# Hybrid encoder block on one core: second token half's transposes placed among the output products of the last chunks, row norms one chunk behind, the last chunk's mixer output gated later

## The chip, the cores and the metric

One core of a Trainium2 chip runs the kernel. The metric is the device time of one execution in microseconds, the median of several runs. The kernel before took 1236.85 us (median of 3 runs, 1236.0 to 1237.21). The trace and the profile page come from one further, profiled execution of the same kernel, which took 1241.54 us.

## The reference, cut to what matters

One layer of an encoder with 1024 tokens of width 1024. Two groups of heads (windowed attention, and gated DeltaNet run forwards and backwards over the tokens) read one normalised input; their outputs are joined, multiplied by `W_out` and added to the input, which gives `h`. Then a feed-forward with a squared ReLU, and a last norm.

```python
attn = _windowed_gqa(...)                       # 8 heads of 64
gdn  = _gdn_mixer(...)                          # rmsnorm(o_fwd + o_bwd) * silu(z), 4 heads of 128
h = h + jnp.concatenate([attn, gdn], axis=-1) @ w_out[l]
hn = _rmsnorm(h, norm_ffn_w[l])
h = h + jnp.square(jax.nn.relu(hn @ w_ffn_in[l])) @ w_ffn_out[l]
return _rmsnorm(h, norm_final_w)
```

## The kernel before

Tokens are handled in 8 chunks of 128, and in two halves of 512: chunks 0 to 3 are the first half, chunks 4 to 7 the second. The kernel is built by a Python class whose generators are woven together. A scheduler in the tile framework then fixes the order of the instructions on each engine once, when the kernel is built; on the chip each engine runs its own list in order and waits at semaphores. Weights and activations are split into a high and a low part, so each product of 128 by 512 takes three matmuls (`mm3`, L125 to L129).

The place of the change is the joint between the mixers and the feed-forward:

- The backward scan (L811 to L862) runs over the chunks from 7 down to 0. When a chunk's scan is done, it is in `self.scanned`.
- `out_gdn(c)` (L905) makes the DeltaNet operand of a chunk: it squares the scan's output by head on ScalarE (L914), turns the sums into a factor on VectorE (L916 to L919) and GpSimd (a power, L920), multiplies (VectorE, L921), transposes four blocks on TensorE (L924, into a `psA` bank), gates with `z` (VectorE, L925) and splits the result in two parts (ScalarE L122, GpSimd L123).
- `out_gemm` (L883) multiplies a chunk's operand by `W_out`: two halves of 12 matmuls each, in a `psA` bank each, and VectorE adds each half to `h[c]` (L890).
- `out_all` (L930) runs over the chunks 7 to 0, keeps up to three chunks' operands ready ahead, and stores `h[c]` to HBM (L940). Chunks are named by their row buffer in listings below.
- `norm_h(c)` (L946) normalises a chunk's row for the feed-forward through `norm_rows` (L199): the square and its sum on ScalarE (L204, 1024 elements), two small operations on GpSimd (L191, L192), and a multiplication on VectorE (L206). The rows of chunks 4 to 7 are scaled in place, after their store to HBM.
- `tokens_second` (L973) normalises chunks 7 to 4 (`norm_half(1)`), and then transposes the second half: for each of 8 blocks of columns, four transposes on TensorE (L210) into one `psB` bank (`token_block`, L954), which ScalarE and VectorE read out as operands (L986, L215, L216, L990, L968, L969). It is woven with the rest of `out_all` once four chunks are summed (L1324).
- After that come the early products of the feed-forward (`early`, L1099: 24 matmuls from the operands of the second half) and `tokens_first` (L999), which transposes the normalised rows of chunks 0 to 3 (L210 again, with `sc` rows) and makes the operands of the first half.
- `psA` and `psB` are two rotations of four PSUM banks each.

Of the kernel before, what the change touches and what calls it, by code (L numbers as in the profile page):

```python
# [22 lines left out]
GH = 4  # L23
# [54 lines left out]
class Block:  # L78
# [46 lines left out]
    def mm3(self, ps, wh, wl, xh, xl, first, last, onto=False):  # L125
        nc = self.nc
        nc.tensor.matmul(ps, wh, xh, start=first, stop=False, skip_group_check=onto)  # L127
        nc.tensor.matmul(ps, wh, xl, start=False, stop=False, skip_group_check=onto)  # L128
        nc.tensor.matmul(ps, wl, xh, start=False, stop=last, skip_group_check=onto)  # L129

# [752 lines left out]
    def out_gemm(self, h, mh, ml, wo):  # L883
        nc = self.nc
        for nh in range(2):
            sl = slice(nh * HALF, (nh + 1) * HALF)
            ps = self.ps("psA")
            for j, k in enumerate((3, 0, 1, 2)):
                self.mm3(ps, mh[:, k, :], ml[:, k, :], wo[k][0][:, sl], wo[k][1][:, sl], j == 0, j == 3)
            nc.vector.tensor_tensor(out=h[:, sl], in0=h[:, sl], in1=ps, op=ALU.add)  # L890
# [14 lines left out]
    def out_gdn(self, c):  # L905
# [16 lines left out]
        ps = self.ps("psA", (P, GH, P))  # L922
        for h in range(GH):
            nc.tensor.transpose(ps[:, h, :], zc[:, 1, h, :], self.ident)  # L924
        nc.vector.scalar_tensor_tensor(out=mix, in0=ps, scalar=self.w_gdn, in1=zc[:, 0], op0=ALU.mult, op1=ALU.mult)  # L925
# [4 lines left out]
    def out_all(self, chunks):  # L930
        while len(self.wo[1]) < 4:
            yield 0.5
        ready = []
        for n, c in enumerate(chunks):
            while c not in self.scanned:
                yield 0.5
            while len(ready) < 3 and n + len(ready) < len(chunks) and chunks[n + len(ready)] in self.scanned:
                ready.append(self.out_gdn(chunks[n + len(ready)]))
            yield from self.out_gemm(self.h[c], *ready.pop(0), self.wo[1])
            self.nc.sync.dma_start(out=self.hd[c], in_=self.h[c])  # L940
            self.summed.append(c)
            if c < 4 and len(self.rows) >= 4:
                self.norm_h(c)

# [9 lines left out]
    def token_block(self, rows, k):  # L954
        ps = self.ps("psB")
        for i in range(4):
            self.transpose_row(rows[i], i, ps, k)
        return ps
# [14 lines left out]
    def tokens_second(self):  # L973


        nc = self.nc
        self.norm_half(1)
        yield 5.0
        rows = [self.rows[4 + i] for i in range(4)]
# [296 lines left out]
    def phases(self):  # L1276
# [40 lines left out]
        def output():  # L1317
# [4 lines left out]
            while len(self.summed) < 4:  # L1322
                yield next(out)
            yield from weave((out, 20.0), (self.tokens_second(), 9.0))  # L1324

# [73 lines left out]
```

## Time and profile before

| what | us |
|---|---|
| median of 3 runs | 1236.85 (1236.0 to 1237.21) |
| the profiled execution | 1241.54 |
| span of its trace | 1239.7 |
| TensorE busy in the span | 1178.8 (95%) |
| VectorE, ScalarE, GpSimd busy | 856.8, 611.3, 560.7 |

The span is the time from the first to the last instruction on the core; the profiled execution is 1.8 us longer than it. TensorE is the busiest engine by far, so what lengthens the program is time in which TensorE waits or runs at a lowered clock. A row of the timeline gives the start in us, the duration in us, the engine, the line, the operation, the tiles written and read, their sizes, how many instructions it merges and, in brackets, how long the engine sat idle before it and what it waited for. A row of the windows gives the stretch, its length, the busy time of each engine with its number of instructions, then the clock that TensorE was granted (1.00 is full), the DMA share and the GB/s.

### The profile page before, as it was taken

Reading aid. Unit: us, or ns where it says so; the run is one execution under the profiler, and the core shown is the slowest. Engines: PE = TensorE matmul, PEld = TensorE weight load, DVE = VectorE, ACT = ScalarE, POOL = GpSimd, SP = SyncE. Lnnn points to the kernel's source line nnn. Section 1 sums busy time; section 2 is a strip of 40 time slices with the busy share of each in tenths; the row PEclk is TensorE's granted clock in tenths of the full one; section 3 lists DMA queues with packets and bytes.
Section 4 is the critical chain, followed back from the end, with each engine's and each line's share of the span. In section 5 each row is a group of like instructions: output and inputs, shape, how many; then the busy total and the mean of one; then the engine's idle time right before and its main releaser. Section 6 shows DMA issues by size and latency. Waiting matters only on the chain. (4 is left out here: it accounts for less than half of the span.)

```text
span 1239.7 us, 18446 instructions
## 1 busy us (share of the span) xinstructions
PE 1178.8 (95%) x6482; PEld 964.3 (78%) x6482; DVE 856.8 (69%) x1482; ACT 611.3 (49%) x1331; POOL 560.7 (45%) x470
## 2 busy tenths in 40 slices
PE   7999999899889999897899999999999999999997
PEld 5788878677768878786788888888777888888885
DVE  4676667993489986776755354453677797887976
ACT  5455688334376761215554454554555433444343
POOL 5354312223321243233673544535446555665595
PEclk9999999899999999999999999999999999999999
DMA  6134344533646576222144434444688624443323
GB/s 241 52 101 144 99 171 143 176 101 112 205 146 184 163 265 248 68 94 91 54 140 158 144 145 159 147 153 144 221 274 298 225 87 155 150 140 133 99 88 136
DMA packets 121629, 187.62 MB, mean 151 GB/s; under 512 B 11043, under 2 KB 64416, under 8 KB 121537
## 3 DMA queue, kind: packets, MB, share of 16 engines
q1 hardware_dynamic: 103876, 155.20, 38.3%
q10 hardware_dynamic: 17661, 31.24, 6.7%
q8 instruction: 51, 0.84, 0.3%
q14 instruction: 41, 0.34, 0.1%
HBM read 122.39 MB, written 63.49 MB: 150 GB/s over the span
## 5 line engine op out<-in xcount | busy, mean ns | idle before, releaser
L127 PE MATMUL psA<-pg,wh 128*128 128x512 f32 x416 | 165.8, 399 | 3.5 <-DVE pt L482 1.9
L129 PE MATMUL psA<-pg,wl 128*128 128x512 f32 x416 | 165.1, 397 | 0.0
L128 PE MATMUL psA<-pg,wh 128*128 128x512 f32 x416 | 165.0, 397 | 0.0
L1174 DVE TENSOR_TENSOR pg<-pg 128x512 fp32r<-128x512 f32 x112 | 121.0, 1114 | 24.8 <-ACT pg L1173 24.8
L123 POOL TENSOR_TENSOR wl<-wr,wh 128x512 fp32r<-128x512 f32 x44 | 66.3, 1527 | 157.3 <-ACT wh L122 129.5
L123 POOL TENSOR_TENSOR wh<-wr,wh 128x512 fp32r<-128x512 f32 x32 | 47.4, 1503 | 128.9 <-ACT wh L122 128.9
L128 PE MATMUL psA<-pg,pg 128*128 128x512 f32 x256 | 100.5, 394 | 2.3 <-POOL pg L123 2.2
L129 PE MATMUL psA<-pg,pg 128*128 128x512 f32 x256 | 100.5, 393 | 0.0
L127 PE MATMUL psA<-pg,pg 128*128 128x512 f32 x256 | 99.6, 394 | 0.9 <-DVE pg L1219 0.8
L1091 ACT ACTIVATE pt<-pt 128x512 f32<-128x512 f32 x64 | 40.3, 632 | 120.6 <-DVE pt L1081 120.6
L123 POOL TENSOR_TENSOR pg<-wr,pg 128x512 fp32r<-128x512 f32 x48 | 72.5, 1540 | 52.7 <-ACT pg L122 48.8
L127 PEld LDWEIGHTS psA<-pg,wh 128*128 128x128 f32 x416 | 79.3, 191 | 21.3 <-ACT pt L464 2.1
L128 PEld LDWEIGHTS psA<-pg,wh 128*128 128x128 f32 x416 | 79.1, 190 | 18.1 <-issue 0.9
L129 PEld LDWEIGHTS psA<-pg,wl 128*128 128x128 f32 x416 | 79.1, 190 | 16.9
L1173 ACT CAST pg<-pg 128x512 fp32r<-128x512 f32 x112 | 67.3, 620 | 40.8 <-DMA pg<-sd 29.3
L128 PE MATMUL psB<-pg,pg 128*128 128x512 f32 x192 | 75.0, 391 | 0.8 <-POOL pg L123 0.7
L129 PE MATMUL psB<-pg,pg 128*128 128x512 f32 x192 | 74.8, 390 | 0.0
L127 PE MATMUL psB<-pg,pg 128*128 128x512 f32 x192 | 74.8, 390 | 0.0
L122 ACT CAST wh<-wr 128x512 fp32r<-128x512 f32 x76 | 43.6, 622 | 52.0 <-PE psA L128 32.0
L1081 DVE TENSOR_TENSOR pt<-psB,pt 128x512 f32<-128x512 f32 x39 | 26.9, 689 | 54.0 <-PE psB L129 29.5
L1081 DVE TENSOR_TENSOR pt<-psA,pt 128x512 f32<-128x512 f32 x39 | 26.8, 689 | 51.7 <-PE psA L129 36.3
L128 PEld LDWEIGHTS psA<-pg,pg 128*128 128x128 f32 x256 | 48.4, 189 | 13.5 <-POOL pg L123 3.7
(395 smaller groups left out, 3244.3 us busy)
## 6 DMA issues: line engine op xcount, KB each, us to landing
sd<-pt ACTq DMA_DIRECT2D x112, 256.0 KB, 2.0
pg<-sd SPq DMA_DIRECT2D x112, 256.0 KB, 2.9
wr<-in_w_ffn_in SPq DMA_DIRECT2D x32, 512.0 KB, 3.6
wr<-in_w_in SPq DMA_DIRECT2D x22, 512.0 KB, 4.8
pg<-in_x SPq DMA_DIRECT2D x16, 512.0 KB, 6.2
wr<-in_w_ffn_out SPq DMA_DIRECT2D x16, 512.0 KB, 4.4
sc<-kvd SPq DMA_DIRECT2D x14, 512.0 KB, 4.1
kvd<-pt SPq DMA_DIRECT2D x16, 256.0 KB, 2.4
```

Source lines behind the costliest of these rows:

```text
L122: nc.scalar.copy(out=h, in_=raw)
L123: (eng or nc.gpsimd).tensor_tensor(out=l, in0=raw, in1=h.bitcast(F32), op=ALU.subtract)
L127: nc.tensor.matmul(ps, wh, xh, start=first, stop=False, skip_group_check=onto)
L128: nc.tensor.matmul(ps, wh, xl, start=False, stop=False, skip_group_check=onto)
L129: nc.tensor.matmul(ps, wl, xh, start=False, stop=last, skip_group_check=onto)
L1081: self.nc.vector.tensor_tensor(out=out, in0=in0, in1=in1, op=ALU.add)
L1091: self.nc.scalar.activation(out=c, in_=c, func=AF.Relu)
L1173: nc.scalar.copy(out=s[:, 0], in_=raw)
L1174: v.tensor_tensor(out=s[:, 1], in0=raw, in1=s[:, 0].bitcast(F32), op=ALU.subtract)
```

## The change

Five edits, all at this joint:

1. `mm3` hands back its last matmul, and `out_gemm` keeps the last matmul of each product it has written in `self.summing`.
2. The transposes of `out_gdn` and those of `token_block` stand in a block that puts them, in TensorE's order alone, behind that last matmul (`issue_after`; on one engine the order is enough, and no semaphore is added).
3. `out_all` normalises the chunk summed before just ahead of a chunk's product, for all chunks. Before, `tokens_second` normalised chunks 7 to 4 in one go, and chunks 3 to 1 were normalised right behind their own sum.
4. `out_all` prepares chunk 0 only while fewer than two operands are ready (three for the other chunks).
5. A new generator `out_and_tokens` takes the place of the weave: behind each half product it takes 0, 1, 2, 2, 2 and 1 steps of `tokens_second`, then the rest. A step is one or the other `token_block` of a pair.

```diff
@@ out_gemm
             for j, k in enumerate((3, 0, 1, 2)):
-                self.mm3(ps, mh[:, k, :], ml[:, k, :], wo[k][0][:, sl], wo[k][1][:, sl], j == 0, j == 3)
+                m = self.mm3(ps, mh[:, k, :], ml[:, k, :], wo[k][0][:, sl], wo[k][1][:, sl], j == 0, j == 3)
+            self.summing = m.ins
@@ out_gdn
-        for h in range(GH):
-            nc.tensor.transpose(ps[:, h, :], zc[:, 1, h, :], self.ident)
+        with self.tc.issue_after(self.summing):
+            for h in range(GH):
+                nc.tensor.transpose(ps[:, h, :], zc[:, 1, h, :], self.ident)
@@ out_all
-        ready = []
-        for n, c in enumerate(chunks):
+        ready, coming = [], list(chunks)
+        for c in chunks:
             while c not in self.scanned:
                 yield 0.5
-            while len(ready) < 3 and n + len(ready) < len(chunks) and chunks[n + len(ready)] in self.scanned:
-                ready.append(self.out_gdn(chunks[n + len(ready)]))
+            while coming and coming[0] in self.scanned and len(ready) < (3 if coming[0] else 2):
+                ready.append(self.out_gdn(coming.pop(0)))
+            if self.summed:
+                self.norm_h(self.summed[-1])
             yield from self.out_gemm(self.h[c], *ready.pop(0), self.wo[1])
             self.nc.sync.dma_start(out=self.hd[c], in_=self.h[c])
             self.summed.append(c)
-            if c < 4 and len(self.rows) >= 4:
-                self.norm_h(c)
+    def out_and_tokens(self, out):
+        tokens, blocks = self.tokens_second(), iter((0, 1, 2, 2, 2, 1))
+        for v in out:
+            yield v
+            if v > 1:
+                yield from itertools.islice(tokens, next(blocks, 0))
+        yield from tokens
@@ token_block
-        for i in range(4):
-            self.transpose_row(rows[i], i, ps, k)
+        with self.tc.issue_after(self.summing):
+            for i in range(4):
+                self.transpose_row(rows[i], i, ps, k)
@@ tokens_second
-        self.norm_half(1)
-        yield 5.0
         rows = [self.rows[4 + i] for i in range(4)]
@@ output
-            yield from weave((out, 20.0), (self.tokens_second(), 9.0))
+            yield from self.out_and_tokens(out)
```

Below are TensorE's rows at the last of the eight column blocks of the second half, before. The `pg` names are the rows of chunks 4, 5, 6 and 7; the L924 row is the four transposes of chunk 0, and the L127 row opens chunk 2's product.

```order
L210 MATMUL psB_6121<-ident,pg_5192 128x128
L210 MATMUL psB_6121<-ident,pg_5096 128x128
L210 MATMUL psB_6121<-ident,pg_5007 128x128
L210 MATMUL psB_6121<-ident,pg_4904 128x128
L924 MATMUL psA_5941<-ident,wr_5926 128x128 x4
L127 MATMUL psA_5951<-pg_5155,pt_5801 128x512
```

Before, all eight blocks stand in one run of 32 transposes, with chunk 0's transposes behind them, and the products of chunks 2, 1 and 0 only after that. In the changed kernel the first block stands between the two halves of chunk 2's product:

```order
L129 MATMUL psA_5925<-pg_4970,pt_5816 128x512
L210 MATMUL psB_5940<-ident,pg_5192 128x128
L210 MATMUL psB_5940<-ident,pg_5096 128x128
L210 MATMUL psB_5940<-ident,pg_5007 128x128
L210 MATMUL psB_5940<-ident,pg_4904 128x128
L127 MATMUL psA_5946<-pg_5155,pt_5815 128x512
```

The other seven blocks follow behind the later half products: two behind chunk 2's second half, two behind each half of chunk 1, one behind chunk 0's first half. Chunk 0's own transposes stand behind the first of these pairs, ahead of chunk 1's product.

The next place is TensorE's list at the transposes of chunk 1, before. The first row ends chunk 4's product, L924 is chunk 1's transposes, the L811 rows are the last of the scan, and the last row opens chunk 3's product.

```order
L129 MATMUL psA_5819<-pg_4970,pt_5691 128x512
L924 MATMUL psA_5850<-ident,wr_5835 128x128 x4
L811 MATMUL psB_5478<-sc_5429,pt_5431 128x128 x2
L811 MATMUL psB_5482<-sc_5340,pg_3716 128x128 x2
L811 MATMUL psB_5487<-sc_5429,pt_5431 128x128 x2
L127 MATMUL psA_5860<-pg_5155,pt_5746 128x512
```

In the changed kernel the scan's rows have moved ahead of chunk 4's product, and chunk 1's transposes (L926 now) stand directly between the two products:

```order
L128 MATMUL psA_5840<-pg_4971,pt_5691 128x512
L129 MATMUL psA_5840<-pg_4970,pt_5692 128x512
L926 MATMUL psA_5871<-ident,wr_5856 128x128 x4
L127 MATMUL psA_5888<-pg_5155,pt_5753 128x512
L128 MATMUL psA_5888<-pg_5156,pt_5753 128x512
```

The third place is VectorE's list for the same transposes, before. `sm` is the small tile of chunk 1's factor, `pg_5096` and `pg_5192` are the rows of chunks 5 and 4, and the L921 row writes what L924 transposes.

```order
L916 TENSOR_TENSOR sm_5837<-sm_5837,sq_1238 128x4
L917 TENSOR_SCALAR sm_5837<-sm_5837 128x4
L890 TENSOR_TENSOR pg_5096<-pg_5096,psA_5764 128x512
L918 RECIPROCAL sm_5837<-sm_5837 128x4
L925 SCALAR_TENSOR_TENSOR wr_5779<-psA_5795,cols,wr_5780 128x512
L919 TENSOR_TENSOR sm_5837<-sm_5837,sq_1238 128x4
L921 TENSOR_TENSOR wr_5835<-dbl_3719,sm_5838 128x512
```

And in the changed kernel, where the lines have moved on by one or two:

```order
L927 SCALAR_TENSOR_TENSOR wr_5793<-psA_5809,cols,wr_5794 128x512
L891 TENSOR_TENSOR pg_5192<-pg_5192,psA_5826 128x512
L206 TENSOR_SCALAR pg_5096<-pg_5096,sm_5820 128x1024
L917 TENSOR_TENSOR sm_5858<-sm_5858,sq_1238 128x4
L918 TENSOR_SCALAR sm_5858<-sm_5858 128x4
L919 RECIPROCAL sm_5858<-sm_5858 128x4
L891 TENSOR_TENSOR pg_5192<-pg_5192,psA_5840 128x512
L920 TENSOR_TENSOR sm_5858<-sm_5858,sq_1238 128x4
L922 TENSOR_TENSOR wr_5856<-dbl_3719,sm_5859 128x512
```

Before, chunk 1's factor and its multiplication stand one chunk earlier, behind the sums of chunk 5 and ahead of those of chunk 4. Now the last small operation (L920) and the multiplication (L922) stand behind the second sum of chunk 4 (the L891 row that reads `psA_5840`), and a row norm (L206) stands among them.

More of the change, by code (lines that the diff above doesn't have):

```diff
@@ L128, in mm3 @@
         nc.tensor.matmul(ps, wh, xl, start=False, stop=False, skip_group_check=onto)
-        nc.tensor.matmul(ps, wl, xh, start=False, stop=last, skip_group_check=onto)
+        return nc.tensor.matmul(ps, wl, xh, start=False, stop=last, skip_group_check=onto)
     def setup(self):
```

## The prediction

> **What bounds the kernel now.** I read the page's head first, then TensorE's timeline at the joint, then windows for its clock.
>
> ```profile
> span 1239.7 us, 18446 instructions
> PE 1178.8 (95%) x6482; PEld 964.3 (78%) x6482; DVE 856.8 (69%) x1482; ACT 611.3 (49%) x1331; POOL 560.7 (45%) x470
> ```
>
> TensorE works 95% of the span, so the program ends earlier only if TensorE loses less time. At the joint it loses a good deal:
>
> ```profile
> 569.07 2.40 PE L210 MATMUL psB<-ident,pg 128*128 128x128 f32 x20 [2.34 <-DVE pg L206]
> 571.95 0.66 PE L210 MATMUL psB<-ident,pg 128*128 128x128 f32 x4 [0.47 <-ACT dbl L986]
> 572.82 0.66 PE L210 MATMUL psB<-ident,pg 128*128 128x128 f32 x4 [0.21 <-DVE dbl L990]
> 574.36 0.63 PE L210 MATMUL psB<-ident,pg 128*128 128x128 f32 x4 [0.88 <-DVE sm L916]
> 578.52 0.93 PE L924 MATMUL psA<-ident,wr 128*128 128x128 f32 x4 [3.54 <-DVE wr L921]
> ...
> 583.38 0.39 PE L127 MATMUL psA<-pg,pt 128*128 128x512 f32 x1
> ...
> 596.77 0.39 PE L129 MATMUL psA<-pg,pt 128*128 128x512 f32 x1
> ...
> 602.90 1.91 PE L210 MATMUL psB<-ident,sc 128*128 128x128 f32 x16
> ```
>
> The brackets are the waits: 2.34 us for the last row norm, then three short ones for read-out of the banks, then 3.54 us for chunk 0's operand; 7.44 us together. Products of three chunks, which need none of this, stand behind in the queue. The wait has a second price, in the clock (the column behind POOL):
>
> ```profile
> 571.83:575.25 3.42, 1.94 (x12) 1.26 (x12) 3.39 (x7) 3.17 (x10) 0.31 (x1) 1.00 0.00 0
> 575.25:578.66 3.41, 0.14 (x1) 0.14 (x2) 2.68 (x6) 0.56 (x2) 1.97 (x2) 1.00 0.00 0
> 578.66:582.07 3.41, 3.41 (x11) 2.82 (x11) 2.67 (x4) 3.02 (x5) 0.65 (x1) 0.52 0.05 10
> 612.79:616.20 3.41, 1.57 (x8) 1.26 (x9) 3.41 (x6) 2.80 (x6) 3.41 (x4) 1.00 0.00 0
> 616.20:619.61 3.41, 3.41 (x9) 2.64 (x9) 2.38 (x5) 3.41 (x7) 3.41 (x3) 0.52 0.00 0
> ```
>
> After a window of 3.41 us with TensorE busy for 0.14 us, the clock is about half for the next 3.41 us, and 1.7 us of work are lost. A window with 1.57 us busy is followed by half clock too, one with 1.94 us isn't. So 1.5 to 1.8 us of idle time in one window are enough.
>
> **The work is the same.** Up to 542.51 TensorE's order is the same in both kernels. From there to 602.90, the first transposition of the first half, both hold the same instructions: 170 matmuls of 512 columns (six chunks of 24, and 26 early ones), 14 scan tiles and 12 groups of four transposes.
>
> ```profile
> 542.51:602.90 60.39, 52.95 (x276) 44.32 (x274) 38.58 (x72) 22.60 (x50) 20.84 (x26) 0.97 0.27 92
> 543.41 1.05 PE L811 MATMUL psB<-sc,sc 128*128 128x128 f32 x8
> 544.30 0.61 PE L811 MATMUL psB<-sc,pg 128*128 128x128 f32 x4
> ```
>
> From 583.38 to 596.77 are 59 steps, 0.227 us each; eight scan matmuls take 0.89 us to the next row, so a tile of four is 0.445 us, and I give a group of four transposes the same. The sum is 170 x 0.227 + 26 x 0.445 = 50.2 us. The stretch took 60.4 us, so before lost 10.2: 7.4 us idle, 1.7 us of half clock, and 1.1 us that the busy column hides (a group behind a wait takes 0.66 us, as its pipeline fills and drains).
>
> **What the change adds: three gates.** With a chunk's operand transposes placed directly between products, the chain that feeds them is no longer covered. Its prices:
>
> ```profile
> 559.09 0.39 PE L129 MATMUL psA<-pg,pt 128*128 128x512 f32 x1
> 559.32 0.60 PE L924 MATMUL psA<-ident,wr 128*128 128x128 f32 x4
> 559.52 0.69 DVE L890 TENSOR_TENSOR pg<-pg,psA 128x512 f32<-128x512 f32 x1 [1.09 <-PE psA L129]
> 560.13 0.75 DVE L925 SCALAR_TENSOR_TENSOR wr<-psA,cols,wr 128x512 f32<-128x512 f32 x1
> ...
> 576.48 0.17 DVE L919 TENSOR_TENSOR sm<-sm,sq 128x4 f32<-128x4 f32 x1
> 576.72 1.02 POOL L920 TENSOR_TENSOR sm<-sm,half_exp 128x4 f32<-128x4 f32 x1 [0.52 <-DVE sm L919]
> 577.77 0.69 DVE L921 TENSOR_TENSOR wr<-dbl,sm 128x512 f32<-128x512 f32 x1 [0.47 <-POOL sm L920]
> ```
>
> TensorE is free at 559.32, the sum starts 0.20 us later, the next VectorE row 0.61 us after that; from the last small operation to the power are 0.24 us, to the multiplication 1.05 us, from there to TensorE (578.52) 0.75 us.
>
> - *Chunk 1.* In the new VectorE order both the last small operation and the multiplication stand behind the second sum of chunk 4, whose product ends directly ahead of the transposes. All five steps lie open: 0.20 + 0.61 + 0.24 + 1.05 + 0.75 = **2.85 us**. Before, this gate cost nothing (559.32 follows 559.09 without a bracket), since factor and multiplication stood a chunk earlier. Behind it in TensorE's queue wait chunk 3's 24 matmuls, though their operand is ready. No semaphore is new; the order alone makes the wait.
> - *Chunk 0.* Only the multiplication stands behind the second sum of chunk 2: 0.20 + 0.61 + 0.75 = 1.56 us, less the eight transposes of two column blocks ahead of it on TensorE (0.89 us): **0.67 us**.
> - *Chunk 2.* Behind chunk 5's last sum stand small operations, two scan corrections, one state term and one output sum, then the multiplication.
>
> ```profile
> 557.25 0.59 DVE L850 SCALAR_TENSOR_TENSOR dbl<-psB,egc,dbl 128x128 f32<-128x128 f32 x2
> 560.79 0.41 DVE L857 TENSOR_TENSOR dbl<-dbl,psB 128x256 f32<-128x256 f32 x1
> 561.12 0.60 DVE L850 SCALAR_TENSOR_TENSOR dbl<-psB,egc,dbl 128x128 f32<-128x128 f32 x2
> ```
>
> From start to start the state pair takes 0.51 us and the output sum 0.33; a correction has the same 256 columns, so 0.33. So 0.81 + 0.66 + 0.51 + 0.33 + 0.2 for small ones + 0.75 = 3.26 us, against six scan tiles on TensorE, 2.67 us: **0.6 us**. Chunk 3's gate is covered by the same six tiles and costs nothing.
>
> The gates make 4.1 us. The gate of chunk 1 leaves TensorE idle for 2.85 us at a stretch; where 1.5 to 1.8 us idle in a window bring the half clock, a gap of 2.85 falls with enough of it into one window in about 8 of 10 positions. I count **1.7 us** for it. The sum is 5.8 us lost where 10.2 were.
>
> **Covered, and counted at nothing.** The 32 transposes no longer wait: rows of chunks 4 to 7 are normalised a product or more ahead. The row norm is also in ScalarE's queue ahead of the next chunk's squares, which delays them:
>
> ```profile
> 550.93 0.31 ACT L914 ACTIVATE scr<-dbl 128x128 f32<-128x128 f32 x1 [3.23 <-DVE dbl L857]
> 551.37 0.31 ACT L914 ACTIVATE scr<-dbl 128x128 f32<-128x128 f32 x1
> 560.91 0.62 ACT L122 CAST pt<-wr 128x512 fp32r<-128x512 f32 x1 [6.60 <-DVE wr L925]
> 561.43 1.05 ACT L204 ACTIVATE pt<-pg 128x1024 bf16<-128x1024 f32 x1
> ```
>
> From chunk 2's transposes on, chunk 1's squares come after 0.7 (transposes) + 0.66 (gating) + 0.52 (split) + 1.05 (norm) + 4 x 0.44 = 4.7 us; with three small operations 5.3 us, against 24 matmuls and the group ahead, 5.9 us: 0.6 us of cover; without it each 0.1 us more is 0.1 us lost. On SP's queue the store of chunk 2 now stands ahead of two weight loads; those issued at 580.72, some 17 us ahead of their first use behind 597.20:
>
> ```profile
> 580.72 2.78 SPq L245 DMA_DIRECT2D wr<-in_w_ffn_in  x2
> 597.20 0.69 DVE L890 TENSOR_TENSOR pg<-pg,psA 128x512 f32<-128x512 f32 x1 [1.36 <-PE psA L129]
> 600.48 2.98 POOL L123 TENSOR_TENSOR wh<-wr,wh 128x512 fp32r<-128x512 f32 x2
> 600.54 1.77 DVE L206 TENSOR_SCALAR sc<-pg,sm 128x1024 f32<-128x1024 f32 x1 [0.72 <-POOL sm L192]
> 602.24 1.77 DVE L1065 TENSOR_TENSOR pt<-wr,pt 128x512 f32<-128x512 f32 x1
> 605.09 1.26 ACT L215 ACTIVATE pg<-psB,cols 128x512 fp32r<-128x512 f32 x2
> ```
>
> The tail from the last sum (597.20) to the first read-out of the first half (605.09) carries on into VectorE, which then works without a pause. In the new order one cast more (0.52 us) stands on ScalarE ahead of that read-out, and GpSimd's second slice no longer runs beside L1065, which may then fall from 1.77 to about 0.7 us. Bounds are +0.5 and -0.6 us; I take 0. Behind that, order and work are the same, so a gain at the joint reaches the end.
>
> **Sum.** 10.2 - 5.8 = 4.4 us. From its own 1241.54 us the profiled execution would come to 1237.1; that lies 4.7 us above the median of the runs, and I move the median by the same 4.4: **1232.4 us**.
>
> **A rule of the skill.** The Trainium skill, "TensorE: Matmul & The Clock Gate", Part 1, says that the array falls to half rate after at least one idle window of about 3.4 us and needs a busy one to recover. The window of 575.25 agrees; that of 612.79, with 1.57 us busy, shows that less than a whole idle window is enough. By the page's words 2.85 us of idle time can't fill a window, and the sum would be 10.2 - 4.1 = 6.1 us; that is the first rival.
>
> **The rivals.**
>
> - *No half clock behind chunk 1's gate.* Gain 10.2 - 4.1 = 6.1 us, 1230.8 us. For it: the gap may straddle two windows. Against it: the row at 612.79. Chance 0.16.
> - *The gates cost more, and nothing is left.* The multiplication and the power have longer forms:
>
> ```profile
> L921 DVE TENSOR_TENSOR wr<-dbl,sm x8: 679/693/1750, 489.6 to 577.8; 128x512 f32<-128x512 f32 x8
> L920 POOL TENSOR_TENSOR sm<-sm,half_exp x8: 1007/1009/1377, 463.2 to 576.7; 128x4 f32<-128x4 f32 x8
> ```
>
>   With 1.06 and 0.37 us more at each gate, 4.3 us go and the time is 1236.7. Against it: in GpSimd's new order no slice of 512 stands beside these multiplications. Chance 0.17.
> - *Slower: VectorE held by GpSimd becomes the bound.* At 600.48 GpSimd works on a slice and the norm at 600.54 takes 1.77 us. In the new order VectorE has row norms, splits and sums of three chunks in a stretch of 23 us, about 17 us of work. If the norms (five) and multiplications (three) each meet a slice and take 1.06 us more, it has 25.5 us of work and TensorE waits 2 to 3 us more, beside the 4.3 us at the gates: about 1239.3. It decides from four long rows on the path (4 x 1.06 against 4.4). Against it: the medians are the short forms, and in the new order GpSimd's next row mostly waits for ScalarE while a norm runs. Chance 0.07. The Trainium skill, "GPSIMD Engine Reference", Key points, says that GpSimd shares its SBUF interfaces with VectorE; the pair at 600.48 and 600.54 agrees.
>
> **Chances.** The forecast itself, 1231.4 to 1233.9, has 0.60. A difference of 0.2%, 2.5 us, is about what a measurement of this kernel can tell from no change, so faster means below 1234.4: the forecast and the first rival, 0.76. Within 0.2% is 0.17, slower 0.07. The range, 1230.0 to 1236.0, takes in the first rival and most of the second.
>
> **What would show it.** Right: no run of 32 transposes; L926 of chunk 1 with a bracket of about 2.7 us for DVE L922, those of chunks 2 and 0 with 0.4 to 0.7, then one window at half clock; the first `sc` transposes about 4.4 us earlier than 602.90. Wrong: brackets on L210 within the products, L926 waiting for ACT rows (the cover of 0.6 us gone), L922 or L206 rows of 1.7 us, or a joint 4 us shorter whose gain is lost behind 620.

## The result, and the profile after

The changed kernel took 1228.78 us (median of 4 runs, 1225.65 to 1231.27), and before, run beside it, 1236.84 us (4 runs, 1236.00 to 1237.21). The ratio is 0.9937 with a 95% interval of 0.9923 to 0.9950, so 6.2 to 9.5 us were gained; the prediction had 4.4 us (1232.4) and a range down to 1230.0. The direction was right, the gain about 1.8 times as large as forecast, and the result 1.2 us below the range. The profiled execution of the changed kernel took 1225.65 us, with a span of 1223.8. A second set of 6 runs gave 1227.32 us and a ratio of 0.9930 (0.9914 to 0.9946).

The page's head of the changed kernel:

```profile
span 1223.8 us, 18442 instructions
PE 1172.2 (96%) x6482; PEld 959.5 (78%) x6482; DVE 858.8 (70%) x1482; ACT 610.7 (50%) x1331; POOL 559.1 (46%) x470
```

TensorE has as many matmuls as before and 6.6 us less busy time: work at half clock counts as longer busy time, and in this execution five half-clock windows fell on TensorE's work, where that of before had nine (1.7 us each if TensorE works throughout). Two of the nine, at 578.76 and 616.31, stand at the joint and at the first half's transposes. The joint, on TensorE's timeline (start, duration, engine, line, operation, tiles, and in brackets the idle time ahead of it):

```profile
549.88 0.66 PE L926 MATMUL psA<-ident,wr 128*128 128x128 f32 x4 [0.27 <-DVE wr L922]
558.75 0.66 PE L926 MATMUL psA<-ident,wr 128*128 128x128 f32 x4 [2.74 <-DVE wr L922]
567.45 0.60 PE L210 MATMUL psB<-ident,pg 128*128 128x128 f32 x4
570.66 1.03 PE L210 MATMUL psB<-ident,pg 128*128 128x128 f32 x8
572.20 0.66 PE L926 MATMUL psA<-ident,wr 128*128 128x128 f32 x4 [0.51 <-DVE wr L922]
575.45 1.03 PE L210 MATMUL psB<-ident,pg 128*128 128x128 f32 x8
```

The three gates are where the prediction put them, chunks 2, 1 and 0 in this order, with 0.27, 2.74 and 0.51 us (forecast 0.6, 2.85 and 0.67). The transposes of the second half have no bracket. So at the joint the mechanism is the one that was forecast. What differs there is the clock. The windows of the clock at chunk 1's gate and at the first half's transposes in this execution (the clock stands behind POOL's count):

```profile
554.16:557.57 3.41, 1.86 (x9) 1.20 (x7) 1.94 (x6) 0.70 (x4) 0.97 (x2) 1.00 0.00 0
557.57:560.99 3.42, 2.24 (x12) 1.93 (x13) 1.45 (x2) 0.76 (x2) 0.46 (x2) 1.00 0.37 153
598.53:601.95 3.42, 1.67 (x13) 1.22 (x11) 3.42 (x6) 3.42 (x7) 3.04 (x3) 1.00 0.26 90
601.95:605.36 3.41, 2.32 (x12) 1.84 (x13) 3.41 (x6) 3.32 (x7) 3.41 (x4) 1.00 0.00 0
605.36:608.77 3.41, 3.41 (x17) 2.83 (x16) 2.20 (x4) 3.41 (x8) 3.41 (x3) 1.00 0.00 0
```

The gap of 2.74 us fell across two windows, 1.86 and 2.24 us of busy time were left in them, and no half clock followed; nor did any follow the first half's transposes, where before had one. The Trainium skill, "TensorE: Matmul & The Clock Gate", Part 1, says that the window of 3413 ns is free-running and doesn't start with the kernel; the traces agree, since the same gap has the windows' edges at other places in other executions (below).

Below, a trace is cut into five parts by the starts of five rows: chunk 7's transposes (the expectations call them the second DeltaNet transposition of the scan's end), chunk 4's transposes, the first `sc` transposes (L210), the first product of the first pair (L127 into `psB`), the end. TensorE's instructions up to chunk 7's transposes are the same in all kernels. Two traces of each kernel, in us:

| part | before | before, second trace | changed | changed, second trace |
|---|---|---|---|---|
| start to chunk 7's transposes | 517.13 | 514.33 | 513.01 | 514.78 |
| scan's end (to chunk 4's) | 18.54 | 18.53 | 17.22 | 17.23 |
| joint (to the first `sc` transposes) | 67.23 | 67.20 | 61.55 | 63.12 |
| first half's blocks (to the first pair) | 12.36 | 12.36 | 11.89 | 11.87 |
| rest | 624.47 | 621.45 | 620.18 | 619.48 |

The first part differs by up to 4.1 us with the same code, so it is no effect of the change. The scan's end gives 1.3 us, the joint 4.1 or 5.7, the blocks 0.5, and the rest the remainder. The second trace of the changed kernel has the half clock behind the gate, the first has not; that is the difference between 5.7 and 4.1.

### The profile page after: what moved, and what is told of

Read it like the earlier page. It is cut to its first block, busy times and chain, and to the rows that moved or that the text cites. A ratio compares the mean times of both kernels' runs of the same rounds, so it can differ in the third digit from the quotient of the medians.

```text
span 1223.8 us, 18442 instructions
## 1 busy us (share of the span) xinstructions
PE 1172.2 (96%) x6482; PEld 959.5 (78%) x6482; DVE 858.8 (70%) x1482; ACT 610.7 (50%) x1331; POOL 559.1 (46%) x470
## 5 line engine op out<-in xcount | busy, mean ns | idle before, releaser
L127 PE MATMUL psA<-pg,wh 128*128 128x512 f32 x416 | 164.9, 397 | 2.3 <-ACT pt L464 2.0
L127 PE MATMUL psA<-pg,pg 128*128 128x512 f32 x256 | 99.0, 391 | 0.9 <-DVE pg L1229 0.9
L127 PEld LDWEIGHTS psA<-pg,wh 128*128 128x128 f32 x416 | 78.7, 189 | 19.7 <-ACT pt L464 2.4
L127 PE MATMUL psB<-pg,pg 128*128 128x512 f32 x192 | 74.7, 389 | 0.0
L127 PEld LDWEIGHTS psA<-pg,pg 128*128 128x128 f32 x256 | 48.0, 188 | 12.6 <-DVE pg L1229 2.1
```

## The experiments

The account to be tested: the extra gain is half-clock windows, which cost 1.7 us each and fall differently in each execution, with 1.3 us at the scan's end. Each expectation puts a theory A that goes with this account against a rival B. All ratios are to runs of before on the same chip in the same session, with 95% intervals. The table gathers what is used below; "hc" is the number of half-clock windows in that part of the kernel's one trace, and a "-" means none. A window that begins at the first half's blocks is counted to the rest, and the half clock at the very end of each trace, where TensorE has no work left, isn't counted.

| kernel | median us | ratio | scan's end | joint | hc | blocks | rest | hc |
|---|---|---|---|---|---|---|---|---|
| before | 1236.84 | | 18.54 | 67.23 | 1 | 12.36 | 624.47 | 2 |
| b0_before | 1235.67 | one run | 18.53 | 67.20 | 1 | 12.36 | 621.45 | 1 |
| changed | 1228.78 | 0.9937 | 17.22 | 61.55 | - | 11.89 | 620.18 | 1 |
| e0_after | 1227.32 | 0.9930 | 17.23 | 63.12 | 1 | 11.87 | 619.48 | - |
| e1_factor_early | 1225.89 | 0.9921 (0.9906 to 0.9936) | 18.54 | 57.24 | - | 11.88 | 622.81 | 2 |
| e2_norms_together | 1235.70 | 0.9991 (0.9978 to 1.0005) | 18.54 | 64.78 | 2 | 13.18 | 621.76 | 2 |
| n1_norms_only | 1230.14 | 0.9953 (0.9940 to 0.9967) | 17.20 | 63.52 | 2 | 12.35 | 622.83 | 2 |
| p11_one_late | 1224.17 | 0.9909 (0.9893 to 0.9925) | 17.23 | 58.96 | - | 11.87 | 620.73 | 1 |
| p0_all_late | 1225.72 | 0.9915 (0.9899 to 0.9930) | 17.22 | 58.20 | - | 12.36 | 621.17 | 1 |
| e1b_factor_early_late_chunks | 1226.38 | 0.9918 (0.9905 to 0.9932) | 17.22 | 57.20 | - | 11.87 | 623.27 | 2 |
| q1_spread | 1225.45 | 0.9912 (0.9897 to 0.9928) | 17.23 | 59.01 | - | 12.84 | 619.27 | - |
| q0_after_spread | 1230.81 | 0.9950 (0.9936 to 0.9965) | 17.22 | 61.53 | - | 12.85 | 621.37 | 1 |
| e3_last_chunk_early | 1231.06 | 0.9953 (0.9939 to 0.9968) | 17.23 | 64.97 | 1 | 11.86 | 621.52 | 1 |
| e4_no_order_block | 1229.30 | 0.9943 (0.9924 to 0.9962) | 17.21 | 62.22 | 1 | 11.88 | 621.36 | 2 |
| q2_spread_copies_late | 1224.65 | 0.9911 (0.9895 to 0.9928) | 17.23 | 58.99 | - | 11.87 | 619.27 | - |
| q3_no_gate_spread | 1224.94 | 0.9898 (0.9881 to 0.9915) | 17.21 | 57.21 | - | 11.87 | 621.62 | 1 |

**The changed kernel again.** No edit.

> The changed kernel again. Theory A (the extra gain of some 3.6 us over the forecast is real and made of three parts: half-clock windows that before always has at the joint and the changed kernel has only in part of its executions, 1.7 us each; 1.3 us at the end of the scan, where VectorE's order also changed; a shorter tail behind the joint): the median comes out at 1227 to 1231 again, executions differ by steps of about 1.7 us, and this trace shows chunk 1's gate at 2.6 to 2.9 us whether or not half clock follows it. Rival B (the first executions were lucky): the median is 1231 to 1234, near the forecast of 1232.4.

The median, 1227.32 us, lies in theory A's range, so the first executions were no luck. The second trace has the same three gates (0.27, 2.74, 0.51), and this time a half-clock window behind chunk 1's. The window that holds the gap, and the two behind it:

```profile
557.28:560.70 3.42, 0.68 (x5) 0.26 (x4) 1.72 (x5) 0.00 (x0) 1.01 (x1) 1.00 0.37 153
560.70:564.11 3.41, 3.41 (x11) 2.82 (x11) 0.75 (x1) 1.67 (x3) 1.11 (x1) 0.50 0.19 56
564.11:567.52 3.41, 3.41 (x16) 2.80 (x16) 1.35 (x2) 0.00 (x0) 0.93 (x3) 1.00 0.07 21
```

The same gap of 2.74 us fell into one window this time, so that 0.68 us of busy time were left. One kernel, two outcomes, 1.6 us apart in the joint.

**Before again.** No edit.

> The kernel before once more, for a second trace. Theory A (TensorE's idle places are fixed by the code, half-clock windows fall differently in each execution, at 1.7 us a window): the stretch from the second DeltaNet transposition of the scan's end to the first half's first transposition again holds the 3.5, 2.3, 0.9, 0.5 and 0.2 us waits and three waits of 0.45 to 1.0 us on VectorE ahead of it, and is 82 to 86 us long; the rest behind it is 631 us plus 1.7 for each half-clock window there, so 633 to 637. Rival B (the first trace of before was an odd one; its losses are not in every execution): one of these waits is missing, or the stretch is below 81 us.

All waits of the first trace are there again (at the joint 2.35, 0.48, 0.21, 0.88 and 3.54 us; at the scan's end 0.44, 0.69 and 0.99), the stretch is 85.7 us as in the first, the half clock follows both the last wait and the first half's blocks. Theory A holds; before's losses are in the code. Its first trace was 3.0 us longer in the rest, of which 1.7 us are one more half-clock window.

**Factors early.** The part of `out_gdn` up to the multiplication (L922) is written a chunk ahead of its transposes, as the order of before had it.

```diff
+    def out_gdn_a(self, c):        # squares, factor, multiplication
...
-                ready.append(self.out_gdn(coming.pop(0)))
+                if half and len(ready) < (3 if half[0][0] else 2):
+                    ready.append(self.out_gdn(*half.pop(0)))
+                else:
+                    half.append(self.out_gdn_a(coming.pop(0)))
```

> The changed kernel, but each chunk's factor and multiplication (L914 to L922) are written one chunk ahead of its transposes, so that no operand chain stands behind the last sum. Theory A: the three gates (2.74, 0.51 and 0.27 us in the trace of the changed kernel) go, and with them the half clock that may follow the first; 3 to 4.5 us faster than the changed kernel, about 1225. Rival B (something else is ready no earlier, the row norms or the read-out of the banks, and takes the gates' place): less than 1.5 us faster.

All three gates are gone and the joint falls to 57.24 us, 4.3 below the first trace of the changed kernel. But the scan's end is 18.54 us again, which gives back 1.3, and the median is only 1.4 us below that of the run beside it. Theory A's size (3 to 4.5 us) was missed, though what it said of the gates is in the trace. The size is that of rival B, but not for its reason: nothing took the gates' place at the joint.

**The scan's end.** This run shows where the 1.3 us come from. VectorE and TensorE there, in the second trace of before:

```profile
522.48 1.24 DVE L917 TENSOR_SCALAR sm<-sm 128x4 f32<-128x4 f32 x1
522.68 0.61 PE L811 MATMUL psB<-sc,pt 128*128 128x128 f32 x4
523.64 0.59 DVE L839 SCALAR_TENSOR_TENSOR sc<-sc,egl,psB 128x128 f32<-128x128 f32 x2
524.15 1.31 DVE L921 TENSOR_TENSOR wr<-dbl,sm 128x512 f32<-128x512 f32 x1
524.28 0.71 PE L811 MATMUL psB<-sc,pg 128*128 128x128 f32 x4 [0.99 <-DVE sc L839]
```

And in the changed kernel:

```profile
520.49 0.68 DVE L1075 TENSOR_TENSOR wr<-wr,wr 128x512 f32<-128x512 f32 x1
520.84 0.61 PE L811 MATMUL psB<-sc,pg 128*128 128x128 f32 x4
521.09 0.59 DVE L839 SCALAR_TENSOR_TENSOR sc<-sc,egl,psB 128x128 f32<-128x128 f32 x2
521.29 0.61 PE L811 MATMUL psB<-sc,pt 128*128 128x128 f32 x4
521.74 0.71 PE L811 MATMUL psB<-sc,pg 128*128 128x128 f32 x4
```

In before a small operation of chunk 3's factor (L917, 128x4) stands ahead of the scan's state term (L839), takes 1.24 us, and TensorE waits 0.99 us for that term. In the changed kernel chunk 3's factor comes later, and the wait is gone. The row of 1.24 us is in before (both traces), in this run and in the next one: each has the wait of 1.0 us and 18.5 us for the scan's end. The other twelve traces have neither, and 17.2 us. The third edit is what moves the factor: with that edit alone the scan's end is 17.20 us, and with all the others but that one 18.54.

**Row norms together again.** The changed kernel with its third edit undone.

```diff
-            if self.summed:
-                self.norm_h(self.summed[-1])
...
+            if c < 4 and len(self.rows) >= 4:
+                self.norm_h(c)
@@ tokens_second
+        self.norm_half(1)
```

> The changed kernel with the row norms put back to where they stood (chunks 7 to 4 together at the start of the second half's transposes, chunks 3 to 1 behind their own sums); transposes stay among the products. Theory A: chunk 1's and 2's gates go (3.0 us), the 1.3 us at the scan's end are lost again, and chunk 0's chain now stands behind four norms and a read-out, a gate of about 5 us with half clock behind it: 1 to 4 us slower than the changed kernel, still 4 to 7 us faster than before. Rival B (the placement among the products is the whole of the gain and the norms' place counts for nothing): within 1 us of the changed kernel.

No gain over before can be measured: the ratio's interval holds 1. Theory A's direction was right, its size too small. Chunk 0's gate grows to 6.38 us, since its factor now stands behind the row norms and the first read-outs, and a window without any work falls into it:

```profile
577.14 1.12 PE L926 MATMUL psA<-ident,wr 128*128 128x128 f32 x4 [6.38 <-DVE wr L922]
```

**Row norms alone.** Before with the third edit only.

```diff
+            if self.summed:
+                self.norm_h(self.summed[-1])
...
-            if c < 4 and len(self.rows) >= 4:
-                self.norm_h(c)
@@ tokens_second
-        self.norm_half(1)
-        yield 5.0
```

> The kernel before with the norms one chunk behind alone: the old weave of transposes and products, no order behind the last matmul, chunk 0 as before. Theory A: the wait of 2.34 us for the last row norm goes, the scan's end gains 1.3 us, chunk 1's gate of 2.7 us comes in, and the runs of transposes still wait for their read-out (1 to 2 us): 1 to 4 us faster than before, 1233 to 1236. Rival B (the norms are the whole of the change): within 1 us of the changed kernel, about 1229.

Theory A had 1233 to 1236, and was missed: this one edit gains 4.1 to 7.4 us. Its scan's end is 17.20 us, and its joint 63.52 us with two half-clock windows in a row, which cost it half of their 2.67 and 3.41 us of busy time:

```profile
558.48 1.12 PE L924 MATMUL psA<-ident,wr 128*128 128x128 f32 x4 [2.74 <-DVE wr L921]
...
567.28 2.35 PE L210 MATMUL psB<-ident,pg 128*128 128x128 f32 x20
```

```profile
554.32:557.74 3.42, 1.43 (x7) 0.85 (x5) 1.93 (x7) 0.32 (x2) 1.01 (x1) 1.00 0.13 54
557.74:561.15 3.41, 2.67 (x9) 2.29 (x10) 1.44 (x2) 0.73 (x2) 0.03 (x1) 0.50 0.24 100
561.15:564.56 3.41, 3.41 (x10) 2.65 (x9) 0.76 (x1) 2.44 (x10) 2.00 (x3) 0.50 0.26 77
```

Without these 3.0 us the joint would be 60.5, about 1 us below the first trace of the changed kernel. The gate of chunk 1 is there too, so it comes from the row norms' new place and not from the queueing. Five column blocks stand in a run, as before, and wait for nothing: once the norms are done a chunk earlier, the run of transposes is no loss.

**The last chunk gated early, and no order block.** The changed kernel with the fourth edit undone, and with the second.

```diff
-            while coming and coming[0] in self.scanned and len(ready) < (3 if coming[0] else 2):
+            while coming and coming[0] in self.scanned and len(ready) < 3:
```

> The changed kernel with the fourth edit undone: chunk 0 is prepared while fewer than three operands are ready, as the other chunks. Its transposes then stand directly between the products of chunks 3 and 2, behind nothing that covers their chain. Theory A (a gate is priced by what lies between it and its chain's start): a second gate of about 2.7 us in place of one of 0.5, and 0 to 3.4 us of half clock behind it: 2 to 5 us slower than the changed kernel, 1230 to 1233. Rival B (the later gating is worth nothing, VectorE has slack there): within 1 us of it, 1227 to 1229.

```profile
561.83 0.66 PE L926 MATMUL psA<-ident,wr 128*128 128x128 f32 x4 [2.74 <-DVE wr L922]
570.23 0.91 PE L926 MATMUL psA<-ident,wr 128*128 128x128 f32 x4 [2.26 <-DVE wr L922]
```

Chunk 0's gate is 2.26 us in place of 0.51 and brought a half-clock window; chunk 1's, with 1.83 us busy in its window, brought none here. Theory A's range (1230 to 1233) holds the median, and its gate of about 2.7 us measured 2.26: in the trace the fourth edit is worth 1.75 us and up to 1.7 of clock. The ratio, 0.9953, is above those of the changed kernel (0.9930 and 0.9937), but the intervals overlap.

```diff
-        with self.tc.issue_after(self.summing):
-            for h in range(GH):
-                nc.tensor.transpose(ps[:, h, :], zc[:, 1, h, :], self.ident)
+        for h in range(GH):
+            nc.tensor.transpose(ps[:, h, :], zc[:, 1, h, :], self.ident)
...
```

> The changed kernel without the blocks that put transposes behind the last written product. The order then differs in one place: two more column blocks of the second half stand ahead of chunk 0's transposes. Theory A: chunk 0's gate of 0.5 us is covered by them (0.9 us), nothing else moves: 0 to 0.7 us faster than the changed kernel. Rival B (the block is what keeps the transposes from standing in a run): waits of 0.5 us or more on read-outs turn up at the four blocks in a row: 0.5 to 2 us slower.

Two more blocks stand ahead of chunk 0's transposes and cover their gate (no bracket); no wait on read-outs turns up. The joint is 0.9 us below that of the second trace of the changed kernel, which also had one half-clock window. The time, 1229.30 us, can't be told from the changed kernel's: the second edit is worth nothing that can be measured.

**Chunk 1's transposes half a product later.** The gate of 2.74 us lies at the end of a chain that the next twelve matmuls could cover.

```diff
+            product = self.out_gemm(self.h[c], *ready.pop(0), self.wo[1])
+            yield next(product)
+            ready = [self.out_gdn_b(*r[1]) if isinstance(r[0], int) else r for r in ready]
+            yield from product
```

`out_gdn_b` is the part of `out_gdn` from the transposes on; it comes late for chunk 1 alone, or for chunks 2, 1 and 0.

> The changed kernel, with chunk 1's transposes (and what follows on them) written behind the first half of chunk 3's product instead of ahead of it; nothing else. Theory A (the gate of chunk 1 is idle time at the end of a chain that the next twelve matmuls would cover): the 2.74 us wait goes, nothing comes in its place, the scan's end keeps its 17.2 us, and no half-clock window follows there: 2.7 us plus up to 1.7 us below the changed kernel, 1223.5 to 1226 where that runs at 1227 to 1229. Rival B (VectorE's work in that stretch is the bound, the gate only shows where it is paid): a wait of 1.5 to 2.7 us turns up at chunk 2's or chunk 1's product or at the first half's transposes, and the time stays within 1 us of the changed kernel.

> The same for chunks 2, 1 and 0: each one's transposes behind the first half of the next product. Theory A: all three gates go (0.27, 2.74 and 0.51 us): 3.5 us plus up to 1.7 us below the changed kernel, 0.5 to 1 below the kernel with chunk 1 alone late, 1222.5 to 1225.5. Rival B: as for chunk 1 alone, or chunk 0's operand comes too late for its product (transposes, gating, split and GpSimd's slice in about 3 us of cover), with a wait of 0.5 us or more ahead of it: no faster than with chunk 1 alone.

With chunk 1 alone the gate is gone, nothing comes in its place, and the time is 1224.17 us, in the range of theory A; the joint is 2.6 us shorter. With all three, all gates are gone, but a weight cast on ScalarE then comes late for an early product (0.68 us at L127), and the blocks take 0.5 us more: 1225.72, just above theory A's range and no faster than with chunk 1 alone, as rival B had it.

**Factors of the late chunks early, scan's end kept.** The edit of the run with early factors, for chunks 2, 1 and 0 alone (`coming[0] < 3` in its condition).

> The changed kernel, with the factor and multiplication of chunks 2, 1 and 0 taken one chunk earlier (as before the change), those of chunks 7 to 3 as changed. Theory A (the factor's place in VectorE's queue makes the gates, and its place at the scan's end made the 1.3 us that the early factor of all chunks gave back): gates gone and the scan's end at 17.2 us: 1.3 us below the earlier run with all factors early (1225.9), 1223.5 to 1225. Rival B (the 1.3 us at the scan's end come from something else): the scan's end is 18.5 us again and the time 1225 to 1227.

The scan's end stays at 17.22 us and the joint is 57.20, the shortest: theory A on both. The time, 1226.38 us, is 1.4 us above theory A's range all the same, and inside rival B's. Its trace loses at the first half's blocks what it gains ahead of them, with two half-clock windows in a row:

```profile
596.20:599.61 3.41, 1.50 (x12) 1.05 (x10) 3.41 (x7) 3.33 (x7) 3.24 (x3) 1.00 0.20 71
599.61:603.03 3.42, 3.00 (x9) 2.27 (x10) 3.42 (x6) 3.41 (x7) 3.42 (x4) 0.50 0.00 0
603.03:606.44 3.41, 3.41 (x10) 2.63 (x9) 1.99 (x3) 3.41 (x7) 3.41 (x4) 0.50 0.00 0
```

**The idle time spread.** A test of the clock itself: at the first half's blocks VectorE's read-outs set the pace, so TensorE's idle time there stays, but it can be spread. The last twelve early matmuls go three behind each of the last four blocks.

```diff
@@ tokens_first, behind the read-outs of block 4 + k
+            self.late(k)
+    def part(self, ps, o, x, k):
+        with self.tc.issue_after(self.turned):
+            self.mm3(ps, o[:, 0, k], o[:, 1, k], x[k][:, 0], x[k][:, 1], k == 0, k == 3)
```

> The kernel with chunk 1 late (1224.2 us), and the last twelve early matmuls, which stood in one run ahead of the first half's last four column blocks, placed three behind each of these blocks. TensorE's work and its idle time of 2.8 us there stay (VectorE's read-outs set the pace), but the idle time is spread, 0.6 to 0.8 us at a time, so that no window of 3.41 us holds more than about 1.5 us of it. Theory A (1.75 us idle in one window brings a window of half clock, which costs 1.7 us): no half-clock window behind these blocks, which every trace but two had so far: 1 to 1.7 us faster, 1222.4 to 1223.3. Rival B (the half clock there costs nothing, since VectorE is the bound, or comes from something else): the same time, 1223.8 to 1225, or the half-clock window is still there.

> The same spreading on the changed kernel itself, nothing else. Theory A: no half-clock window behind the first half's blocks; the two traces of the changed kernel had none there either, but its runs vary from 1225.2 to 1231.6, so part of them has: 0 to 1.2 us faster than the changed kernel, 1226 to 1228. Rival B: no change, 1227 to 1229, or slower, where the two copies that ScalarE now makes ahead of the fifth block's read-out hold it up.

In both traces the first of the four waits is 0.34 or 0.38 us and the others 0.65, and no half clock follows them. From the first pair to the end, the first of them takes 619.27 us, where chunk 1 late alone took 620.73. But the pair starts 1.0 us later, and neither kernel got faster, so theory A was missed in both (1222.4 to 1223.3 and 1226 to 1228); the second one is if anything slower than the changed kernel (0.9950 against 0.9930 and 0.9937, with intervals that overlap). The cause of the later pair, in the first of the two: a copy on ScalarE ahead of the fifth block's read-out (L215), VectorE's wait for it, and TensorE's for VectorE.

```profile
600.62 0.59 ACT L1110 COPY pt<-psA 128x512 f32<-128x512 f32 x1
601.62 0.70 ACT L215 ACTIVATE pg<-psB,cols 128x512 fp32r<-128x512 f32 x1
602.35 0.75 DVE L216 SCALAR_TENSOR_TENSOR pg<-psB,cols,pg 128x512 fp32r<-128x512 f32 x1 [0.95 <-ACT pg L215]
603.90 0.47 PE L127 MATMUL psB<-pg,wh 128*128 128x512 f32 x1 [1.03 <-DVE pt L1045]
```

So the copies were left behind, on the kernel with chunk 1 late and on the one with early factors:

```diff
@@ early
-        x7 = self.copied(d)
@@ pair_products
+            x7 = self.copied(d)
```

> The kernel with chunk 1 late and the last early matmuls spread, with the copies of the early product taken in the pair instead of ahead of it, so that ScalarE reads out the fifth block first. Theory A (a half-clock window costs the end 1.7 us; the two copies cost 1.0): the first pair product 88.0 to 88.2 us after the second DeltaNet transposition of the scan's end, as with chunk 1 late alone, no half-clock window there, and from the pair to the end 619.3 as in the run with the early copies, where chunk 1 late alone had 620.7: a span 1.0 us below the run with the early copies and 1.4 to 1.7 below chunk 1 late alone, 1222 to 1224. Rival B (VectorE is the bound from there on, the clock is not): from the pair to the end 620.7 us or more, 1224 to 1226.

> The same spreading with late copies on the kernel whose factors of chunks 2, 1 and 0 are early (1226.4 us, no gate left; its trace had 6.8 us of half clock at the first half's blocks). Theory A: its stretch from the second DeltaNet transposition to the first half's first transposition stays at 74.4 us, and the half clock goes: 1.7 to 3.4 us below 1226.4, 1222 to 1224.5, the fastest of all. Rival B: 1225 to 1227, the half clock was off the path.

The first does in its trace what theory A said, to 0.1 us: the pair comes 88.09 us after chunk 7's transposes, no half clock follows, and the rest takes 619.27 us. From chunk 7's transposes on, this trace and that of chunk 1 late alone differ by one half-clock window and by 1.43 us, 1.46 of them in the rest: in this pair of traces that is what the window cost the end. In the medians (1224.65 and 1224.17 us) it doesn't show; theory A's 1222 to 1224 was missed, and the median lies in rival B's range; a difference of 1.5 us lies within the spread of single runs, 1223.54 to 1228.41 for the two. The second has the lowest ratio of all, 0.9898, but its interval overlaps that of chunk 1 late alone; 1224.94 us lies above theory A's range, though no half clock follows the blocks in its trace. That the spreading keeps the half clock away is seen in four traces of four; that it makes the program faster is not shown.

Over all sixteen traces the rest of the program takes 619.3 us without a half-clock window (three traces), 621.1 with one (mean of seven, 620.18 to 621.62), 622.4 with two (mean of five, 621.36 to 623.27), and 624.5 in the first trace of before, with two and a load that came 1.1 us late. Not all of these windows stand behind the blocks: eight traces, the first of the changed kernel among them, have one that begins between 880 and 896 us. TensorE waits there for ScalarE in before too (1.37 and 2.16 us in its second trace), but neither trace of before has that window, and what decides on it was not tried.

## Why the prediction was off, by its own steps

- *What bounds the kernel.* Right. TensorE's idle time at the joint was a loss of 7.4 us in both traces of before. Of chunk 0's wait 0.51 us is left, of the others nothing.
- *Up to 542.51 TensorE's order is the same.* True, and the step that failed first: the same order isn't the same time. VectorE's order differs from about 520 on, and with it a wait of 1.0 us goes. 1.3 us of the gain lie ahead of the stretch that the prediction priced, which put them at nothing. The shift of chunk 3's factor was visible in VectorE's order, which the prediction read only at chunk 1's transposes.
- *The three gates.* Right in place, cause and size: 3.5 us measured, 4.1 forecast. The chain of 2.85 us measured 2.74.
- *The half clock behind chunk 1's gate.* Counted in full, 1.7 us, though the prediction itself gave it 8 of 10 positions. Of the six traces with this gate three have it (the second of the changed kernel, row norms alone, no order block) and three don't. With it the joint gained 4.1 us, where 4.4 was the forecast; without it 5.7, where the first rival had 6.1. Both were sized well; the truth is a mixture. At the prediction's own 8 of 10 the term would have been 1.4 us, at three of six it is 0.85, and six traces are few.
- *Behind that, a gain at the joint reaches the end.* The step that failed second. It reached the end, but more came: the first half's blocks take 0.5 us less (the estimate of -0.6 to +0.5 held this), and the half clock behind them became less certain. The 0.5 us came by another row than the prediction named. The additional cast stands on ScalarE as it said, but L1065 (L1075 now) keeps its 1.77 us; it is the row norm ahead of it that fell from 1.77 us to 0.75:

```profile
589.39 0.75 DVE L206 TENSOR_SCALAR sc<-pg,sm 128x1024 f32<-128x1024 f32 x1
590.05 1.77 DVE L1075 TENSOR_TENSOR pt<-wr,pt 128x512 f32<-128x512 f32 x1
```

  The first of TensorE's three waits at these blocks, before and in the changed kernel:

```profile
611.97 0.63 PE L210 MATMUL psB<-ident,sc 128*128 128x128 f32 x4 [1.28 <-DVE pt L1013]
600.30 0.63 PE L210 MATMUL psB<-ident,sc 128*128 128x128 f32 x4 [0.73 <-DVE pt L1023]
```

  Before has that half clock in both traces, as have the three other traces in which the first of the three waits there is 1.18 us or more; where that wait is 0.7 us, as in the changed kernel, four traces of seven have it. The prediction had this window's row in hand (612.79, 1.57 us busy), used it as evidence on the clock, and didn't ask whether the change would move it.
- *The sum.* Forecast 4.4. By the runs: 4.1 at the joint with the half clock, 0.85 for the half of executions without it, 1.3 at the scan's end, 0.5 at the blocks, and 1.7 x 3/7 = 0.7 for their half clock: 7.5 us, where 6.2 to 9.5 were measured.
- *Queueing the transposes.* The prediction priced the change as one piece. Taken apart, the third edit, the row norms, carries most of it (0.9953 alone, 0.9991 for the rest without it), the fourth 1.75 us and its clock beside the others, and the second nothing that shows. The fifth was not tried alone. What the other four edits add to the third, which alone has 0.9953, is not clear of noise: the changed kernel has 0.9930 and 0.9937, with intervals that overlap. So a gain from placing the transposes among the products, beyond the row norms' new place, is not shown.
- *Rivals.* Gates that cost more, and VectorE held up by GpSimd: neither is seen at the joint, where the L922 rows take 0.7 us. Rows lengthened beside a GpSimd slice do appear at the scan's end, in both kernels (L922 with 1.63 and 1.24 us in the changed one); the one that cost a wait at the state term, L917 with 1.24 us, is of the two kernels in before alone. No rival allowed for a gain above 6.1 us.

What stays open: the difference of the medians, 8.06 us in the first set and 9.74 in the second, is 0.6 to 2.2 us above the 7.5 that are accounted for; the share of executions with each window is known from a few traces only, and the windows that begin at 880 to 896 us are not in the sum.

## What to carry to other kernels

When a change reorders one engine, compare the order of every engine from the first row that moves, not from where the bottleneck's order changes: the place of a 128x4 operation on VectorE was worth 1.3 us. Price the clock as a chance for each gap, before and after, at every later place that the shift touches, since where a gap falls among the windows differs from one execution to the next. And when a chain is exposed at a gate, try placing the waiting instruction half a product later: one edit of a few lines took 1224.17 us, 12 us less than the runs of before beside it, and 3 to 4.6 us less than the two medians of the changed kernel. (Those were measured in other sessions, and the intervals of the ratios still overlap a little; that the gate is gone is plain in the trace.)

## What was not expected of the hardware

- **The threshold for half clock lies at about half a window.** Of the windows measured between 545 and 625 us, each with 1.58 us of busy time or less was followed by half clock, and none with 1.71 us or more; between lie 1.62 and 1.67 without and 1.68 with it (the last is the window that the prediction cut at 612.79; the windows' edges are known to about 0.1 us). Elsewhere in the traces the line is less sharp: a window with 1.52 us (from 329.96, early factors for the late chunks) and one with 1.57 us (from 888.38, the changed kernel's second trace) were not followed by half clock, and one with 1.84 us (from 215.71, all three chunks late) was. The Trainium skill, "TensorE: Matmul & The Clock Gate", Part 1, has a whole idle window as the condition; the measurements decide otherwise.
- **The way back has a threshold too.** In the same stretch a half-clock window with 3.00 us of busy time or less was followed by another one (the windows of 557.74 and 599.61 above), one with 3.06 us or more by full clock, as here with chunk 1 late alone. This line isn't sharp either: in the same trace a half-clock window from 341.39 with 2.92 us was followed by full clock.

```profile
604.21:607.63 3.42, 3.08 (x7) 2.49 (x8) 2.82 (x5) 3.42 (x8) 3.42 (x4) 0.50 0.00 0
607.63:611.04 3.41, 3.41 (x16) 2.82 (x15) 2.38 (x3) 3.41 (x8) 3.41 (x4) 1.00 0.02 5
```

- **A small operation can be held for seven times its length.** L917 on 128x4 mostly takes 0.17 us in the second trace of before, and took 1.24 us at 522.48, while GpSimd worked on a slice from 522.03 to 523.70. In the sixteen traces 40 of VectorE's 512 small operations on the factors (128x4) take over 0.3 us. Each of the 40 began while GpSimd worked on a slice of 128x512 and ended 0.02 to 0.03 us after that slice. The reciprocals (0.17 us) that began beside a slice were not lengthened.

```profile
522.03 1.67 POOL L123 TENSOR_TENSOR pt<-wr,pt 128x512 fp32r<-128x512 f32 x1 [2.96 <-ACT pt L122]
```
